# Two fp32r matmuls on the high and low parts of the sums of squares in place of one fp32 matmul

## The chip, the cores and the metric

The kernel runs on one core of a Trainium2 chip. The metric is the time of one execution on the device in microseconds (us); before the change three timed runs gave 1935.99, 1937.84 and 1938.87 us, median 1937.84. The engines are TensorE (PE, matmuls; its weight loads are listed as PEld), VectorE (DVE), ScalarE (ACT), GpSimd (POOL) and SyncE (SP), which issues most DMA transfers.

## The reference, cut to what matters

One decoder layer for 1024 prompt tokens and 64 sample tokens, width 1024: two SwiGLU feed-forward networks (FFN), and between them a mixer of windowed attention and a gated linear recurrence. Each of the three parts has a norm before it and a norm behind it, and all are root-mean-square norms:

```python
def rms_norm(x, g):
    xf = x.astype(jnp.float32)
    y = xf * lax.rsqrt(jnp.mean(xf * xf, axis=-1, keepdims=True) + EPS)
    return (y * g.astype(jnp.float32)).astype(x.dtype)

def run_layer(x, ...):
    x = x + 0.5 * rms_norm(swiglu(rms_norm(x, norm_ffn1_pre), ffn1_w_gu, ffn1_w_down), norm_ffn1_post)
    h = rms_norm(x, norm_mix_pre)
    ...
    x = x + rms_norm(mix, norm_mix_post)
    x = x + 0.5 * rms_norm(swiglu(rms_norm(x, norm_ffn2_pre), ffn2_w_gu, ffn2_w_down), norm_ffn2_post)
```

## The kernel before

The tokens are cut into three groups: group 0 has 320 (256 prompt tokens and the 64 samples), groups 1 and 2 have 384 each. Each large product is made of three matmuls (`mm3`, lines 260 to 262): a number is split into a high part of the type fp32r and the fp32r rest, and high times high, high times low and low times high are added up in a bank of PSUM. `split` (lines 238 to 241) makes the parts: a cast on ACT for the high one, a subtraction on DVE (or POOL) for the low one. Weights arrive in raw tiles over SP's queue and are split the same way.

Group 0 is kept feature-major for most of the program, with features on the partitions and tokens in the columns, and so are groups 1 and 2 before the first FFN. There a norm has to sum over partitions. `bcast_steps` (line 313) squares the eight blocks of 128 features on ACT and adds them up on DVE (on POOL for groups 1 and 2) in a tile `ss` of 128 rows; `mean_root` (line 290) multiplies `ss` by `omean`, a matrix that holds 1/1024 everywhere, which gives every partition the mean of all squares, and takes the root's inverse with a few steps on DVE and ACT (lines 297 to 305). The matmul by `omean` is an fp32 one (line 295). It stands at eight places: in the opening (`pre_first`, group 0), in the two norms of groups 1 and 2 before the first FFN (`pre_x`), behind and before the first FFN and the mixer (`post_t`, `pre_t`, group 0, four places) and at the end (`post_t`).

What sets the order: the norms' code runs as generators in named streams. `tick()` is called after each piece of a product and lets a stream go on to its next `yield`, so the number of `yield`s sets between which products a step of a norm stands; `need(name)` runs a stream to its end. The code written so is then put in order engine by engine by a scheduler that works with its own time simulation. In `pre_first` the order of the opening is written by hand: `order` and `after` chain the instructions of an engine. The small tiles (`ss`, `sq`, `rt`, `mt`, `mq`, and those of the gates, `sg` and `su`) share a ring of eight buffers with the tag "t2".

The opening makes six products of 320 columns with weights 0 to 5; their banks are read by `gated0` (lines 718 and 725) as soon as the root `rb` is there. Up to 138 us the gate and up products of group 0 follow, and beside them `factor` (lines 469 and 471) makes the operands of the two other groups for a multiplication of seven instead of eight products. The second matmul of the FFN for groups 1 and 2 starts about 570 us (weights `w`, activations `ar`), and beside it the stream `c0` runs `post_t` and `pre_t` for group 0, with residual sums on POOL (line 349).

Of the kernel before, what the change touches and what calls it, by code (L numbers as in the profile page):

```python
# [8 lines left out]
F32 = mybir.dt.float32  # L9
F32R = mybir.dt.float32r  # L10
# [4 lines left out]
ALU = mybir.AluOpType  # L15
# [3 lines left out]
P = 128  # L19
D = 1024  # L20
# [27 lines left out]
def tile_step(ctx: ExitStack, tc: tile.TileContext, A: dict, O: list):  # L48
    nc = tc.nc
    V, S, G, PE = nc.vector, nc.scalar, nc.gpsimd, nc.tensor  # L50

    cp = ctx.enter_context(tc.tile_pool(name="cp", bufs=1))
    pp = ctx.enter_context(tc.tile_pool(name="pp", bufs=1))
# [5 lines left out]
    def uid(s):  # L59
        cnt[0] += 1  # L60
        return f"{s}_{cnt[0]}"
# [4 lines left out]
    def axbank(s="ax"):  # L66
        return ps.tile([P, 512], F32, tag="ax", bufs=4, name=uid(s))
# [55 lines left out]
    ones = cp.tile([P, P], F32, name="ones")  # L123
    V.memset(ones, 1.0)
    junk = cp.tile([P, 512], BF16, name="junk")
    omean = cp.tile([P, P], F32, name="omean")
    V.memset(omean, 1.0 / D)
    S.activation(junk[:, :P], ones, AF.Silu)
    cols = cp.tile([P, NROWS], F32, name="cols")
    f1pre = cp.tile([P, KC], F32, name="f1pre")  # L130
# [106 lines left out]
    made = {}  # L237

    def split(hi, lo, src, lo_eng=None):
        made['S'] = S.copy(hi, src).ins  # L240
        (lo_eng or V).tensor_tensor(lo, src, hi.bitcast(F32), op=ALU.subtract)  # L241
# [16 lines left out]
    def mm3(out, a, b, first, last, resume=False):  # L258

        PE.matmul(out, a[0], b[0], start=first, stop=False, skip_group_check=resume)  # L260
        PE.matmul(out, a[0], b[1], start=False, stop=False, skip_group_check=resume)  # L261
        return PE.matmul(out, a[1], b[0], start=False, stop=last, skip_group_check=resume).ins  # L262
# [24 lines left out]
    def tmp2(name, shape=(P, 512)):  # L287
        return pp.tile(list(shape), F32, tag="t2", bufs=8, name=uid(name))

    def mean_root(ss, dst=None):  # L290
        w = ss.shape[-1]
        bank = axbank("rb")
        y = tmp2("rt")[:, :w]
        x = bank[:, :w]
        made = PE.matmul(x, omean, ss, start=True, stop=True)
        t = tmp2("mt")[:, :w]
        V.tensor_scalar(y.bitcast(I32), x.bitcast(I32), -0.5, float(MAGIC), op0=ALU.mult, op1=ALU.add)
        S.activation(t, y, AF.Square)
        V.tensor_tensor(t, x, t, op=ALU.mult)
        V.scalar_tensor_tensor(y, t, -3.0 * RS ** 2, y, op0=ALU.add, op1=ALU.mult)  # L300
        S.activation(t, y, AF.Square)
        V.tensor_tensor(t, x, t, op=ALU.mult)
        q = tmp2("mq")[:, :w]
        V.scalar_tensor_tensor(q, t, -40.0 / 3 * RS ** 6, t, op0=ALU.add, op1=ALU.mult)
        end = V.scalar_tensor_tensor(x if dst is None else dst, q, 80.0 * RS ** 12, y, op0=ALU.add, op1=ALU.mult)
        return made, x, end

    def sum_squares(E, ss, sq, d):
        if d == 1:
            return V.scalar_tensor_tensor(ss, ss, EPS * D / P, sq, op0=ALU.add, op1=ALU.add)  # L310
        return E.tensor_tensor(ss, ss, sq, op=ALU.add)

    def bcast_steps(part, w, out, add=None):

        ss = tmp2("ss")
        for d in range(KC):
            if d == 0:
                S.activation(ss[:, :w], part(d), AF.Square)
                continue
            sq = tmp2("sq")  # L320
            S.activation(sq[:, :w], part(d), AF.Square)
            sum_squares(G if add else V, ss[:, :w], sq[:, :w], d)
            if d % 3 == 0 or add:
                yield
        yield
        if add:
            yield
            yield
        rb = mean_root(ss[:, :w])[1]
        yield  # L330
        yield
        out.append(rb)
        yield
# [248 lines left out]
    def pre_first(x, gpre, h, raws, wts):  # L582
# [3 lines left out]
        w = WIDTH[0]  # L586
# [8 lines left out]
        def order(e, made):  # L595
            last[e] = made.ins
            return made

        def after(e):
            return tc.issue_after(last[e]) if e in last else nullcontext()  # L600
# [23 lines left out]
        def products(bank, n, ks):  # L624
            for k in ks:
                with after("PE"):
                    last["PE"] = mm3(bank[:, :w], (tiles[n][0][:, k, :], tiles[n][1][:, k, :]), hcol(h[0], k, w),
                                     k == 0, k == KC - 1)

        ss = tmp2("ss")[:, :w]  # L630

        def squares(ds):
            for d in ds:
                sq = tmp2("sq")[:, :w] if d else ss
                with after("S"):
                    order("S", S.activation(sq, x_part(d), AF.Square))
                if d:
                    with after("V"):
                        order("V", sum_squares(V, ss, sq, d))
# [18 lines left out]
        squares(range(2, 5))  # L658
        weight(4, 0, KC)
        squares(range(5, 8))  # L660
        products(banks[1][0], 2, range(KC))
        products(banks[1][1], 3, range(7))
        weight(5, 0, KC)
        rb = tmp2("rb")[:, :w]
        with after("PE"), after("V"), after("S"):
            made = mean_root(ss, rb)
        order("PE", made[0])
        order("V", made[2])
        products(banks[1][1], 3, range(7, KC))
# [1245 lines left out]
```

## Time and profile before

| | us |
|---|---|
| timed runs, median (lowest to highest) | 1937.84 (1935.99 to 1938.87) |
| profiled execution: span from first to last instruction | 1937.4 |
| PE busy | 1923.1 |
| PE's weight loads busy | 1806.1 |
| DVE busy | 1430.7 |
| ACT busy | 946.0 |
| POOL busy | 186.1 |

For the profiled execution the span is the only time that is recorded. The page cuts the span into 40 equal slices:

```profile
PE   9999999999999999999999999999999999999998
DVE  6896789877568666787678758756987887656666
ACT  5553444444455434545445545846544444445452
PEclk9999999999999999999999999999999999999999
```

Each digit is the busy share of a slice in tenths (9 is 90% or more); PEclk is the clock granted to TensorE, in tenths of its full speed. PE is busy from end to end at full clock. Matmuls are pipelined, and their recorded durations overlap: what one costs in a stream is read from the start of one to the start of the next.

### The profile page before, as it was taken

The numbers are of one execution on the slowest core, as the hardware profiler recorded it, in microseconds if no ns is written. First come the engines' busy times: TensorE is split into PE (matmuls) and PEld (weight loads), VectorE is DVE, ScalarE is ACT, GpSimd is POOL, SyncE is SP. The second block draws the span as 40 slices with busy tenths as digits, with TensorE's granted clock in tenths as the row PEclk, the third lists the DMA queues.
The fourth block names the chain that finished last, engine by engine and source line by source line (L and its number), as shares of the span: only waits on it lengthen the run. The fifth ranks groups of instructions, "written<-read, shape, count | busy, mean of one in ns | idle before, by whom it ended". The sixth has DMA issues, their size and how long they took to land.

```text
span 1937.4 us, 34843 instructions
## 1 busy us (share of the span) xinstructions
PE 1923.1 (99%) x13547; PEld 1806.1 (93%) x13547; DVE 1430.7 (74%) x2469; ACT 946.0 (49%) x1701; POOL 186.1 (10%) x227
## 2 busy tenths in 40 slices
PE   9999999999999999999999999999999999999998
PEld 9999999999998987788999888989999999999886
DVE  6896789877568666787678758756987887656666
ACT  5553444444455434545445545846544444445452
POOL 0300000000004022020221212000000000000102
PEclk9999999999999999999999999999999999999999
DMA  6643676555767556765334344546555555667974
GB/s 248 209 133 115 232 267 247 206 191 184 242 217 242 180 155 215 283 220 163 114 102 153 99 140 142 164 147 209 185 198 192 198 188 189 210 228 241 308 255 141
DMA packets 175750, 375.56 MB, mean 194 GB/s; under 512 B 16144, under 2 KB 67536, under 8 KB 175568
## 3 DMA queue, kind: packets, MB, share of 16 engines
q1 hardware_dynamic: 169680, 362.84, 56.0%
q10 hardware_dynamic: 5904, 10.49, 1.5%
q8 instruction: 106, 1.74, 0.4%
q14 instruction: 60, 0.49, 0.1%
HBM read 290.86 MB, written 83.39 MB: 193 GB/s over the span
## 4 chain that ended last, share of the span: by engine, by line
PE 88%; DMA 6%; DVE 3%; ACT 1%; issue 1%; POOL 1%; SPq 0%; ACTq 0%; DVEq 0%; POOLq 0%
PE mm L260 27%; PE mm L262 26%; PE mm L261 26%; DMA ar<-fa 1%; DMA xt<-in_x_rest_dram 1%; DMA ar<-act 1%; PE lv L1337 1%; PE sc L1237 1%; DMA raw<-in_ffn_w_gu_dram 1%; PE pv L1283 1%; DVE w L241 1%; PE pT L1269 1%; PE c L262 0%; PE c L260 0%; PE c L261 0%
## 5 line engine op out<-in xcount | busy, mean ns | idle before, releaser
L260 PE MATMUL mm<-h,wsph 128*128 128x320 f32 (+1 forms) x1344 | 427.2, 319 | 0.4 <-DVE big L814 0.4
L261 PE MATMUL mm<-h,wsph 128*128 128x320 f32 (+1 forms) x1344 | 425.5, 317 | 0.2 <-DVE h L241 0.2
L262 PE MATMUL mm<-h,wspl 128*128 128x320 f32 (+1 forms) x1344 | 422.6, 316 | 0.0
L241 DVE TENSOR_TENSOR wspl<-raw,wsph 128x1024 fp32r<-128x1024 f32 x208 | 260.8, 1255 | 125.2 <-ACT wsph L240 124.1
L240 ACT CAST wsph<-raw 128x1024 fp32r<-128x1024 f32 x208 | 217.8, 1049 | 254.0 <-PE mm L261 199.3
L260 PEld LDWEIGHTS mm<-h,wsph 128*128 128x128 f32 x1344 | 252.2, 188 | 4.2 <-issue 2.3
L261 PEld LDWEIGHTS mm<-h,wsph 128*128 128x128 f32 x1344 | 252.5, 188 | 3.9 <-issue 2.3
L262 PEld LDWEIGHTS mm<-h,wspl 128*128 128x128 f32 x1344 | 251.9, 188 | 3.4 <-issue 3.1
L240 ACT CAST w<-raw 128x512 fp32r<-128x512 f32 (+1 forms) x208 | 153.8, 745 | 199.9 <-PE mm L261 96.2
L261 PE MATMUL mm<-h,w 128*128 128x384 f32 (+1 forms) x736 | 245.6, 334 | 0.3 <-DVE h L622 0.3
L260 PE MATMUL mm<-h,w 128*128 128x384 f32 (+1 forms) x736 | 245.7, 334 | 0.2 <-ACT h L620 0.2
L262 PE MATMUL mm<-h,w 128*128 128x384 f32 (+1 forms) x736 | 239.6, 333 | 0.5 <-POOL w L613 0.4
L241 DVE TENSOR_TENSOR w<-raw,w 128x512 fp32r<-128x512 f32 (+1 forms) x208 | 178.3, 861 | 72.6 <-ACT w L240 71.7
L261 PE MATMUL mm<-w,h 128*128 128x512 f32 x462 | 180.5, 391 | 0.7 <-DVE w L241 0.7
L260 PE MATMUL mm<-w,h 128*128 128x512 f32 x462 | 180.8, 394 | 0.0
L262 PE MATMUL mm<-w,h 128*128 128x512 f32 x462 | 179.8, 391 | 0.0
L260 PE MATMUL mm<-big,w 128*128 128x384 f32 x528 | 176.7, 335 | 0.3 <-ACT big L806 0.2
L261 PE MATMUL mm<-big,w 128*128 128x384 f32 x528 | 176.5, 334 | 0.0
L262 PE MATMUL mm<-big,w 128*128 128x384 f32 x528 | 176.0, 334 | 0.0
L261 PEld LDWEIGHTS mm<-h,w 128*128 128x128 f32 x736 | 138.1, 188 | 1.1 <-DVE h L622 0.8
L260 PEld LDWEIGHTS mm<-h,w 128*128 128x128 f32 x736 | 138.1, 188 | 0.8 <-ACT h L620 0.5
L262 PEld LDWEIGHTS mm<-h,w 128*128 128x128 f32 x736 | 137.6, 188 | 1.0 <-POOL w L613 0.7
(367 smaller groups left out, 3353.8 us busy)
## 6 DMA issues: line engine op xcount, KB each, us to landing
raw<-in_ffn_w_gu_dram SPq DMA_DIRECT2D x162, 512.0 KB
raw<-in_ffn_w_down_dram SPq DMA_DIRECT2D x74, 512.0 KB
raw<-in_w_in_dram SPq DMA_DIRECT2D x54, 512.0 KB
ar<-fa SPq DMA_DIRECT2D x70, 384.0 KB
big<-in_ffn_w_down_dram SPq DMA_DIRECT2D x88, 256.0 KB
fb<-big SPq DMA_DIRECT2D x44, 512.0 KB
fa<-big SPq DMA_DIRECT2D x22, 768.0 KB
raw<-fb SPq DMA_DIRECT2D x30, 512.0 KB
```

Of the source, the lines that this page charges most:

```text
L240: made['S'] = S.copy(hi, src).ins
L241: (lo_eng or V).tensor_tensor(lo, src, hi.bitcast(F32), op=ALU.subtract)
L260: PE.matmul(out, a[0], b[0], start=first, stop=False, skip_group_check=resume)
L261: PE.matmul(out, a[0], b[1], start=False, stop=False, skip_group_check=resume)
L262: return PE.matmul(out, a[1], b[0], start=False, stop=last, skip_group_check=resume).ins
L1237: PE.matmul(banks[g][rows(hq), i, cs], zq[rows(g), 2 * pr + i, b * P + 64 * hq:b * P + 64 * hq + 64], kx[rows(g), k0 + cs.start:k0 + cs.st ...
L1269: PE.transpose(tb2[hq][:, g, i, slot], pt[g][rows(hq), c:c + P], ident[rows(hq), rows(hq)])
L1283: PE.matmul(ob[par][rows(g), :, hq], vn[rows(par), b + (blk + hq) // 2, rows(g)], pT[hq][rows(par), g, :, PLACE[hq][blk]], start=alone or ...
L1337: PE.matmul(b5[32 * i:32 * i + 32, b, a], K[:, a, cs], Q[:, a, cs], start=True, stop=True)
```

## The change

`omean` gets the type fp32r. The sums `ss` are split into two fp32r parts `ms`, a cast on ACT and a subtraction on DVE, and two matmuls by `omean` add both into the same bank. In `bcast_steps` the split stands one step behind the last square, and the matmuls two or three steps behind the split: each norm has one `yield` more before its matmul. In the opening the split is written behind the last square and ahead of the products with weights 2 and 3 in the code's order; on ACT and DVE it so comes ahead of the sixth weight tile (number 5).

```diff
-    omean = cp.tile([P, P], F32, name="omean")
-    V.memset(omean, 1.0 / D)
+    omean = cp.tile([P, P], F32R, name="omean")
+    V.memset(omean.bitcast(F32), 1.0 / D)
...
-    def mean_root(ss, dst=None):
-        w = ss.shape[-1]
+    def mean_parts(w):
+        return [pp.tile([P, 512], F32R, tag="t2", bufs=8, name=uid("ms"))[:, :w] for _ in range(2)]
+
+    def two_parts(ss):
+        parts = mean_parts(ss.shape[-1])
+        split(*parts, ss)
+        return parts
+
+    def mean_root(parts, dst=None):
+        w = parts[0].shape[-1]
         bank = axbank("rb")
         y = tmp2("rt")[:, :w]
         x = bank[:, :w]
-        made = PE.matmul(x, omean, ss, start=True, stop=True)
+        PE.matmul(x, omean, parts[0], start=True, stop=False)
+        made = PE.matmul(x, omean, parts[1], start=False, stop=True)
...
             if d % 3 == 0 or add:
                 yield
+        if add:
+            yield
+        parts = two_parts(ss[:, :w])
+        yield
         yield
         if add:
             yield
-            yield
-        rb = mean_root(ss[:, :w])[1]
+        rb = mean_root(parts)[1]
...
         squares(range(5, 8))
+        with after("S"):
+            order("S", S.copy(parts[0], ss))
+        with after("V"):
+            order("V", V.tensor_tensor(parts[1], ss, parts[0].bitcast(F32), op=ALU.subtract))
         products(banks[1][0], 2, range(KC))
         products(banks[1][1], 3, range(7))
         weight(5, 0, KC)
         rb = tmp2("rb")[:, :w]
         with after("PE"), after("V"), after("S"):
-            made = mean_root(ss, rb)
+            made = mean_root(parts, rb)
```

The scheduler then places instructions anew. PE keeps its other instructions, and their order up to small shifts of the attention's pieces among the products. Two places are shown, one row for an instruction (or several alike), in the order of the engine. The first is DVE in the opening, from the last three sums of squares (`ss`) on; `w_313` is the low part of the sixth weight tile, `rt` the first step of the root. Before:

```order
L311 TENSOR_TENSOR ss_146<-ss_146,sq_258 128x320
L311 TENSOR_TENSOR ss_146<-ss_146,sq_261 128x320
L311 TENSOR_TENSOR ss_146<-ss_146,sq_264 128x320
L613 TENSOR_TENSOR w_313<-big_109,w_312 128x1024
L145 TENSOR_SCALAR halfpost<-cols 128x8
L146 TENSOR_SCALAR halfpost<-cols 128x8
L150 TENSOR_SCALAR nsinkb<-nsinkb 128x8
L201 TENSOR_TENSOR lbe<-cols 128x4
L297 TENSOR_SCALAR rt_318<-rb_317 128x320
```

With the change (its lines are numbered anew: 320 is the old 311, 625 the old 613, 306 the old 297):

```order
L320 TENSOR_TENSOR ss_146<-ss_146,sq_260 128x320
L320 TENSOR_TENSOR ss_146<-ss_146,sq_263 128x320
L320 TENSOR_TENSOR ss_146<-ss_146,sq_266 128x320
L677 TENSOR_TENSOR ms_148<-ss_146,ms_147 128x320
L145 TENSOR_SCALAR halfpost<-cols 128x8
L146 TENSOR_SCALAR halfpost<-cols 128x8
L150 TENSOR_SCALAR nsinkb<-nsinkb 128x8
L201 TENSOR_TENSOR lbe<-cols 128x4
L202 TENSOR_TENSOR lbe<-cols,lbe 128x4
L203 TENSOR_TENSOR lbe<-cols,lbe 128x4
L625 TENSOR_TENSOR w_317<-big_109,w_316 128x1024
L306 TENSOR_SCALAR rt_322<-rb_321 128x320
```

The subtraction `ms` has come between the sums and the small constants, and the sixth weight tile's low part, which stood before those constants, now stands right ahead of the root's first step.

The second place is ACT about 580 to 592 us, where the second matmul of the first FFN runs: `w` are casts of its weights, `h` of its activations, `ss` and `sq` the squares of the norm `pre_t`, which wait for POOL's residual sums. Before:

```order
L240 CAST h_6177<-ar_6178 128x2x384
L240 CAST w_6034<-raw_6032 128x1024
L318 ACTIVATE ss_6021<-big_5069 128x320
L240 CAST h_6214<-ar_6215 128x384
L321 ACTIVATE sq_6023<-big_5069 128x320
L321 ACTIVATE sq_6026<-big_5069 128x320
L321 ACTIVATE sq_6029<-big_5069 128x320
L321 ACTIVATE sq_6055<-big_5070 128x320
L240 CAST w_6087<-raw_6085 128x1024
L240 CAST h_6243<-ar_6244 128x2x384
L321 ACTIVATE sq_6058<-big_5070 128x320
L1014 COPY big_5802<-mm_5803 128x512
```

With the change (327 and 330 are the old 318 and 321, 1031 the old 1014):

```order
L240 CAST w_6041<-raw_6039 128x1024
L310 ACTIVATE mt_5939<-rt_5936 128x320
L240 CAST h_6231<-ar_6232 128x384
L240 CAST w_6098<-raw_6096 128x1024
L240 CAST h_6268<-ar_6269 128x2x384
L1031 COPY big_5817<-mm_5818 128x512
L1031 COPY big_5817<-mm_5819 128x512
L240 CAST w_6141<-raw_6139 128x1024
L1031 COPY big_5817<-mm_5820 128x512
L240 CAST h_6297<-ar_6298 128x2x384
L327 ACTIVATE ss_6064<-big_5084 128x320
L330 ACTIVATE sq_6066<-big_5084 128x320
```

Before, five squares stood ahead of the cast of `w_6087`; now the cast that answers to it, `w_6098`, and the next one, `w_6141`, stand ahead of the first square.

## Rows read from the trace of the kernel before

**Rows 1.** The page's first lines: span, and busy time of each engine.
```profile
span 1937.4 us, 34843 instructions
...
PE 1923.1 (99%) x13547; PEld 1806.1 (93%) x13547; DVE 1430.7 (74%) x2469; ACT 946.0 (49%) x1701; POOL 186.1 (10%) x227
```

**Rows 2.** The page's chain of waits, by engine and by line.
```profile
PE 88%; DMA 6%; DVE 3%; ACT 1%; issue 1%; POOL 1%; SPq 0%; ACTq 0%; DVEq 0%; POOLq 0%
PE mm L260 27%; PE mm L262 26%; PE mm L261 26%; DMA ar<-fa 1%; DMA xt<-in_x_rest_dram 1%; DMA ar<-act 1%; PE lv L1337 1%; PE sc L1237 1%; DMA raw<-in_ffn_w_gu_dram 1%; PE pv L1283 1%; DVE w L241 1%; PE pT L1269 1%; PE c L262 0%; PE c L260 0
```

**Rows 3.** Who PE waited for: us in total, times, longest.
```profile
PE spT L1517 <- ACT t L1512: 1.3, 1, 1.3
...
PE mm L261 <- DVE w L241: 0.7, 1, 0.7
```

**Rows 4.** The group of the tile omean: minimum, median, maximum in ns.
```profile
L295 PE MATMUL rb<-ss,omean x16: 430/432/590, 22.0 to 1780.9; 128*128 128x320 f32 x12, 128*128 128x384 f32 x4
```

**Rows 5.** Timeline of PE at 94 us: start, duration, engine, line, operation.
```profile
94.17 0.31 PE L262 MATMUL mm<-h,wspl 128*128 128x320 f32 x1
...
95.11 0.31 PE L261 MATMUL mm<-h,wsph 128*128 128x320 f32 x1
95.26 0.31 PE L262 MATMUL mm<-h,wspl 128*128 128x320 f32 x1
```

**Rows 6.** Timeline of PE at 1009 us.
```profile
1009.16 0.34 PE L260 MATMUL mm<-h,wsph 128*128 128x384 f32 x1
...
1010.05 0.33 PE L262 MATMUL mm<-h,wspl 128*128 128x384 f32 x1
1010.22 0.34 PE L260 MATMUL mm<-h,wsph 128*128 128x384 f32 x1
```

**Rows 7.** Groups by line: a DVE subtraction's like, and ACT's cast.
```profile
L311 DVE TENSOR_TENSOR ss<-ss,sq x36: 480/492/1157, 16.4 to 1774.8; 128x320 f32<-128x320 f32 x36
...
L240 ACT CAST h<-ht x16: 438/459/461, 609.2 to 1085.3; 128x320 fp32r<-128x320 f32 x16
```

**Rows 8.** Timelines of POOL and PE: w_in's operand, last piece and first reader.
```profile
619.83 0.87 POOL L241 TENSOR_TENSOR h<-ht,h 128x320 fp32r<-128x320 f32 x1
...
634.94 0.30 PE L260 MATMUL mm<-h,wsph 128*128 128x320 f32 x1
```

**Rows 9.** Timelines of DVE and PE in the opening.
```profile
19.09 1.68 DVE L311 TENSOR_TENSOR ss<-ss,sq 128x320 f32<-128x320 f32 x3
...
22.73 0.49 DVE L297 TENSOR_SCALAR rt<-rb 128x320 int32<-128x320 int32 x1 [0.53 <-PE rb L295]
...
27.98 0.48 DVE L718 TENSOR_TENSOR sg<-mm,rb 128x320 f32<-128x320 f32 x1
...
30.00 0.31 PE L260 MATMUL mm<-h,wsph 128*128 128x320 f32 x1
```

**Rows 10.** Timeline of PE's weight loads at 56 us, with what was waited for.
```profile
56.61 0.30 PEld L295 LDWEIGHTS rb<-ss,omean 128*128 128x128 f32 x2 [0.31 <-POOL ss L311]
```

**Rows 11.** Timelines of ACT, DVE and PE around 592 us.
```profile
589.23 0.47 ACT L321 ACTIVATE sq<-big 128x320 f32<-128x320 f32 x1 [0.68 <-POOL big L349]
...
590.67 1.53 DVE L241 TENSOR_TENSOR w<-raw,w 128x1024 fp32r<-128x1024 f32 x1 [1.13 <-ACT w L240]
...
590.89 0.39 PE L262 MATMUL mm<-w,h 128*128 128x512 f32 x1
591.12 0.39 PE L260 MATMUL mm<-w,h 128*128 128x512 f32 x1
592.25 0.50 PE L261 MATMUL mm<-w,h 128*128 128x512 f32 x1 [0.74 <-DVE w L241]
```

**Rows 12.** Busy time in a stretch: us, then each engine (instructions), clock, DMA.
```profile
110.00:140.00 30.00, 30.00 (x204) 30.00 (x203) 30.00 (x35) 16.54 (x21) 0.00 (x0) 1.00 0.44 134
```

**Rows 13.** Timelines of DVE and PE: the first weight after the gate phase.
```profile
134.40 1.29 DVE L241 TENSOR_TENSOR w<-raw,w 128x512 fp32r<-128x512 f32 x2
...
137.79 0.34 PE L260 MATMUL mm<-h,w 128*128 128x384 f32 x1
```

More of the change, by code (lines that the diff above doesn't have):

```diff
@@ L630, in pre_first @@
         ss = tmp2("ss")[:, :w]
+        parts = mean_parts(w)
         def squares(ds):
```

## The prediction

> **What bounds the kernel now.** I read the page's top first. The span is 1937.4 us and TensorE (PE) is busy for 1923.1 us of it [rows 1]; the reader is to see that nothing but TensorE's own stream can be shortened much. The chain of waits then puts 88% of the span on PE, nearly all of it the three-matmul products on lines 260 to 262 [rows 2]. The list of waits of PE is short: its longest single item is 1.3 us, and one of 0.7 us stands near a place of this change [rows 3]. So a microsecond counts only if it is taken out of PE's stream, or if a late operand puts a hole into it.
>
> The changed operation is one matmul, line 295, at eight places; the group by tile shows 16 records, two per place, of 430 to 590 ns [rows 4]. Records overlap, so I price it from start to start in the timeline. At 94 us the three-term stream of 320 columns runs at 0.147 us a matmul (95.11 to 95.26). The matmul of line 260 stands between the one of line 262 at 94.17 and the one of line 261 at 95.11: 0.94 us for two steps of 0.147, so line 295, 384 columns wide here, took 0.94 - 0.29 = 0.65 us [rows 5]. At 1009 us the same reading of a 320-column one, between products of 384 columns at 0.172 us a step, is 1010.05 - 1009.16 - 2 x 0.172 = 0.545 us [rows 6]. The other five 320-column places (22, 573, 600, 1055 and 1780 us) read alike give 0.535 to 0.55 us; the second 384-column place (56 us) has a wait in it and is priced like that of 94 us.
>
> **The change, part by part.** *The matmuls.* Each place loses 0.545 us (six times) or 0.65 us (twice) and gains two fp32r matmuls. Their kind, 128x128 weights with 320 or 384 columns in fp32r, is that of the stream around them: 0.147 or 0.172 us each [rows 5, 6]. Saved: 6 x (0.545 - 0.294) + 2 x (0.65 - 0.344) = 1.51 + 0.61 = 2.12 us, all on the path. The bounds of this term: no saving at all if a pair cost what the one did, and 2.2 us with the largest readings of line 295 (0.55 and 0.65) and the smallest of a step (0.144 and 0.17).
>
> The row says that the fp32 matmul costs 0.545 us against 0.147 us, a factor of 3.7. The Trainium skill, "FP8 and Floating Point Precision", section TensorE Precision Notes, says that a true fp32 product is made in four passes through the array, and a reduced fp32 in one. Four full steps would be 0.588 and 0.688 us, and the term would be 2.45 us instead of 2.12; I keep the measured start-to-start.
>
> *The splits.* Eight casts on ScalarE (ACT), about 0.46 us each at 320 columns, and eight subtractions on VectorE (DVE), about 0.49 us each [rows 7]: 3.7 and 3.9 us on engines that are busy 49% and 74% of the span [rows 1]. They lengthen each norm's chain by some 1.1 us with two hand-offs, and the streams give each norm one more step before the matmul. What hides this is the distance from a norm to its reader. For the norm before w_in, the last low part leaves POOL about 620.7 and PE first reads this tile at 634.94 [rows 8], 14 us; the printed order puts the second norm's matmul 35 to 42 products later than before, which at 0.23 us a product of 512 columns [rows 11] is up to 9.7 us. It still fits, by some 4 us; what didn't fit would be PE's wait. The norm before the second FFN has more room still by the same reading. The last norm, at 1780 us, feeds only an output.
>
> *The opening.* This is the tightest place. The sum of squares is complete at 20.77 us [rows 9]; then cast (0.09 hand-off + 0.46), hand-off 0.09 and subtraction 0.49 end at 21.9. PE comes to the first new matmul at 21.99 and to the second at 22.13, so it shouldn't wait; that is 0.2 us of room. But ACT now casts the sums before the sixth weight tile, and DVE subtracts before that tile's low part, as the order shows. So this 1.04 us cast starts at 21.3, the 1.22 us subtraction at about 22.4, and the first step of the root (line 297, in order behind it on DVE) starts at 23.6 instead of 22.73: 0.85 us late. Everything behind on DVE moves as well, and the first reading of a product's bank (line 718) goes from 27.98 to 28.8, ending at 29.3. The product that takes this bank next starts at 30.00, after the change at 29.75. There is 0.45 us left, and I cost this at nothing; every microsecond more on DVE's queue would be 0.5 us or more of PE waiting.
>
> *A wait that goes.* At 56 us PE's weight load waited 0.31 us for the POOL sum [rows 10]. The order now puts the first part 18 products (2.6 us) later, the second 27 products. The wait goes: -0.31 us.
>
> *A wait that may go.* At 592 us PE stands 592.25 - 591.12 - 0.23 = 0.90 us for the low part of a weight tile [rows 11]. Its cast stood on ACT behind five squares of a norm, which waited for POOL's residual sums. In the new order two weight casts more stand ahead of those squares, but the residual's loads stand behind one more load of right-hand sides on SP. I count this as zero, with bounds of -0.9 and +0.9 us.
>
> *Everything else* (one constant tile's type, two more buffers of the "t2" ring, the attention pieces shifted by 2 to 18 products) keeps the number and order of PE's other instructions. Zero, and I allow 1 us either way, the size of the longest waits there [rows 3].
>
> Sum: 2.12 + 0.31 = 2.43 us. Against the profiled execution's span this is 1937.4 - 2.4 = 1935.0; no time around the span is given for it, and the three timed runs (1935.99 to 1938.87) enclose it, with a median 0.44 us above. Taken from the median: **1935.4 us**, 0.13% less.
>
> **Rivals.** *A larger gain.* The wait at 592 us goes too: 2.43 + 0.90 = 3.3 us, 1934.5. For it: the casts' new place in ACT's order; against: the later loads on SP, and that squares now stand ahead of a later cast.
>
> *No gain from the swap.* Two accumulating matmuls of another kind of number could cost what the two records of the fp32 one do (0.43 us each, overlapping). Then only the 0.31 us is left: 1937.5. For it: the fp32 matmul is two loads and two matmul records already [rows 4], so the count of records doesn't fall. Against: fp32r pairs run at 0.147 us everywhere else in the trace.
>
> *VectorE's backlog, the case of slower.* From 110 to 140 us DVE is busy for 30.00 of 30.00 us [rows 12]: it makes the FFN's operand sums and their low parts, behind the second prompt norm at 94 us. That norm's matmul moves 24 products (3.5 us) later; less what is saved until then, the root starts some 2.9 us later, and DVE has two subtractions of 384 columns more, at most 0.6 us each (0.49 by 384/320). The first weight of the next phase is split on DVE at 134.40 and ready about 135.0; PE wants it at 137.79 [rows 13], 2.8 us of room. If all 2.9 + 1.2 = 4.1 us arrived there and DVE's queue behind it had no room either, PE would stand for 4.1 us in all: 4.1 - 2.4 = 1.7 us slower, 1939.5. It decides from the point where DVE's pieces for the next phase come more than 2.8 us later than before. Against it: the new order moves the last operand's split and one eviction behind this weight, and takes one weight split and two gate products ahead of the root; by my count of the queue the weight is ready no later than before.
>
> **How the numbers follow.** The forecast (1935.4, give or take 1) has 0.52, the larger gain 0.24, no gain from the swap 0.12, the backlog 0.12. About 0.2%, 3.9 us, is what a measurement of this kernel can tell from no change. Faster by more than that is under 1934.0: two fifths of the larger gain and a sixth of the forecast, 0.19. Slower by more is over 1941.7, which takes the backlog and 2 us of small waits on top: 0.05. Within: 0.76. The range: 1932.6 (the larger gain, 1 us of small waits fewer, and the 1 us by which the three runs lie around their median) to 1939.9 (the backlog and half a microsecond of these).
>
> **What would show it.** Right: line 295's sixteen records of 0.43 us and more are replaced by sixteen of 0.31 to 0.34 us, and PE takes 0.25 to 0.31 us less per place from start to start; no wait of PE on the new tile "ms"; the wait on POOL at 56 us is gone; PE's busy time falls by about 2 us. Wrong: PE waiting for line 675 or 677 at 22 us or for a bank at 29.8 us; PE waiting for weights or operands between 137 and 150 us; a new hole between 575 and 620 us; or more than 0.4 us from start to start for a pair.

## The result, and the profile after

| | before | after |
|---|---|---|
| median of the timed runs, us | 1937.34 (1935.99 to 1939.32, 14 runs) | 1942.44 (1938.12 to 1945.74, 14 runs) |
| span of the profiled execution, us | 1937.4 | 1940.2 |

The ratio after to before is 1.0023, 95% interval 1.0016 to 1.0031: about 4.5 us slower by the ratio, 5.1 between the medians. The forecast was 1935.4, with 1939.9 as the upper end of the range. The sign was wrong. The changed kernel's runs also spread over 7.6 us, those of the kernel before over 3.3. Where a run has both, the time is 1.7 us more than the span (1941.87 and 1940.2 for the profiled execution of the changed kernel); by this the profiled execution of before took an estimated 1939.1 us, 1.8 above its median, and that of the changed kernel is 0.6 below its own. The two traces so show 2.8 us of the 5.1.

The place of the gain and of the loss can be read by following one instruction through both traces. The rows are the starts of the first matmul of a stretch, which does the same work in both kernels; what changes from row to row was won or lost between them, in one execution of each.

| first matmul of | before, us | after, us | difference |
|---|---|---|---|
| the gate stage's last operand sums | 130.46 | 129.58 | -0.88 |
| the last change of operands ahead of the down products | 516.07 | 513.87 | -2.20 |
| w_in for the samples [rows 8] | 634.94 | 631.45 | -3.49 |
| the down products after it | 684.54 | 685.99 | +1.45 |
| the down products after the second w_in | 1135.20 | 1138.65 | +3.45 |
| the last of the FFN's head | 1389.40 | 1392.38 | +2.98 |

So up to 631 us the changed kernel was 3.5 us ahead, more than I had forecast for the whole program. 4.9 us were then lost between 635 and 685 us, and another 2 us between 685 and 1135 us.

Not all of the 3.5 us is the change's. 1.3 us of it were won between 130 and 516 us, where no changed matmul stands: short waits of PE in the trace of before (0.17 us for line 806 at 305.69, 0.18 for line 241 at 486.62 and 0.44 for line 814 at 496.31, and a step 0.3 us too long at 291) are gone or shorter. The two profiles of e2 below, one kernel, have some of them in one and fewer in the other, so they come and go with the execution.

*What was won.* The page's top answers to [rows 1]; the span has grown by 2.8 us and PE is busy 1.5 us longer, where I had forecast about 2 us less.

```profile
span 1940.2 us, 34852 instructions
...
PE 1924.6 (99%) x13547; PEld 1809.1 (93%) x13547; DVE 1434.9 (74%) x2477; ACT 948.4 (49%) x1709; POOL 193.4 (10%) x227
```

PE's timeline at 22 us (320 columns) and at 97 us (384 columns, [rows 5]) shows the pairs: start, duration, engine, line, operation.

```profile
22.26 0.31 PE L303 MATMUL rb<-ms,omean 128*128 128x320 f32 x1
...
22.55 0.31 PE L260 MATMUL mm<-h,w 128*128 128x320 f32 x1
...
97.26 0.34 PE L303 MATMUL rb<-ms,omean 128*128 128x384 f32 x1
...
97.61 0.31 PE L260 MATMUL mm<-h,wsph 128*128 128x320 f32 x1
```

A pair takes 22.55 - 22.26 = 0.29 us and 97.61 - 97.26 = 0.35 us from start to start, as forecast. Before, one matmul took 0.545 and 0.65 us.

*The first loss.* Who PE waited for [rows 3] now begins with a wait that was not there:

```profile
PE mm L260 <- DVE big L1028: 3.2, 1, 3.2
```

Line 1028 (1011 before) is the eviction (the reading of a bank, which frees it) of the three banks of the down product with number 6 of seven: `V.tensor_tensor(y1[1][:, i], bank, y1[0][:, i], op=ALU.add)`. The product ring has four banks; w_in's first projection takes the fourth, its second needs the first of these three. PE's timeline there, and the granted clock by stretches (us, busy us, instructions, weight loads, VectorE, ACT, POOL, then the clock):

```profile
634.82 0.31 PE L262 MATMUL mm<-h,wspl 128*128 128x320 f32 x1
638.29 0.61 PE L260 MATMUL mm<-h,wsph 128*128 128x320 f32 x1 [3.16 <-DVE big L1028]
638.70 0.47 PE L261 MATMUL mm<-h,wsph 128*128 128x320 f32 x1
...
641.82 0.31 PE L261 MATMUL mm<-h,wsph 128*128 128x320 f32 x1
```

```profile
635.00:640.00 5.00, 1.84 (x7) 1.74 (x7) 3.53 (x6) 3.89 (x7) 0.00 (x0) 0.83 0.66 224
640.00:645.00 5.00, 5.00 (x30) 5.00 (x30) 5.00 (x7) 4.62 (x9) 1.22 (x1) 0.83 0.77 232
```

The step into 638.29 is 3.47 us instead of 0.147, 3.32 us lost. Behind it the matmuls start 0.266 us apart instead of 0.147: TensorE runs at the lower of its two levels (1.2 instead of 2.4 GHz; the mean of these two stretches is 0.83, and 1.00 in the one before and the one behind) until about 641.7. From 638.29 to 641.82 there are 13 steps; at 0.147 they would take 1.91 us and not 3.53, another 1.62 us. Together 4.9 us, the whole of the first loss.

*Why the eviction was late.* VectorE, ACT, POOL and SP of the changed kernel in the 35 us before, one fence each:

```profile
617.45 0.96 DVE L241 TENSOR_TENSOR h<-ar,h 128x768 fp32r<-128x768 f32 x1 [4.52 <-ACT h L240]
...
620.05 3.76 DVE L379 SCALAR_TENSOR_TENSOR ht<-big,cols,rb 128x320 f32<-128x320 f32 x8
...
629.96 1.62 DVE L241 TENSOR_TENSOR h<-ar,h 128x768 fp32r<-128x768 f32 x1
...
636.59 0.96 DVE L241 TENSOR_TENSOR h<-ar,h 128x768 fp32r<-128x768 f32 x1 [1.47 <-ACT h L240]
637.46 0.68 DVE L1028 TENSOR_TENSOR big<-mm,big 128x512 f32<-128x512 f32 x1
```

```profile
616.58 0.83 ACT L240 CAST h<-ar 128x768 fp32r<-128x768 f32 x1 [6.84 <-DMA ar<-fa]
617.32 0.47 ACT L310 ACTIVATE mt<-rt 128x320 f32<-128x320 f32 x1
...
635.72 0.83 ACT L240 CAST h<-ar 128x768 fp32r<-128x768 f32 x1 [2.32 <-DMA ar<-fa]
```

```profile
623.41 9.75 POOL L241 TENSOR_TENSOR h<-ht,h 128x320 fp32r<-128x320 f32 x7
```

```profile
607.22 1.72 SPq L1103 DMA_DIRECT2D aon<-in_attn_out_norm_dram  x1
609.00 0.43 SPq L1105 DMA_DIRECT2D bhi<-in_b_in_dram  x1
609.51 0.38 SPq L1015 DMA_DIRECT2D ar<-fa  x1
```

And of the kernel before, ACT and then VectorE:

```profile
604.43 0.47 ACT L301 ACTIVATE mt<-rt 128x320 f32<-128x320 f32 x1
```

```profile
608.58 3.75 DVE L367 SCALAR_TENSOR_TENSOR ht<-big,cols,rb 128x320 f32<-128x320 f32 x8
...
633.93 0.96 DVE L241 TENSOR_TENSOR h<-ar,h 128x768 fp32r<-128x768 f32 x1 [1.91 <-ACT h L240]
634.81 0.68 DVE L1011 TENSOR_TENSOR big<-mm,big 128x512 f32<-128x512 f32 x1
```

PE's timelines of the matmuls of this norm, before and then after, show how little of the delay is the place:

```profile
600.13 0.70 PE L295 MATMUL rb<-ss,omean 128*128 128x320 f32 x2
```

```profile
604.50 0.31 PE L303 MATMUL rb<-ms,omean 128*128 128x320 f32 x1
...
606.26 0.31 PE L304 MATMUL rb<-ms,omean 128*128 128x320 f32 x1
```

The reader is to see a chain. The norm's matmuls come 4.4 and 6.1 us later, but its second square (line 310; 301 before) is at 617.32 instead of 604.43, 12.9 us later: it now stands behind a cast of a right-hand side (`ar`) in ACT's order, whose load was issued behind two others and kept ACT standing for 6.84 us. That cast itself is 2.3 us later than before (616.58 against 614.26) and 0.5 to 2.3 later than in e1, e2 and e3 below, where the square stands ahead of it. The norm's eight results leave VectorE at 620 to 624 instead of 609 to 612 us, and their low parts keep POOL busy without a break from 623.4 to 633.2. In that time VectorE's subtraction of 768 columns takes 1.62 us instead of 0.96. VectorE gives the raw buffers back later, SP loads later, and the fifth right-hand side, behind which the eviction stands in both orders, is cast at 635.72 instead of 633.05. The eviction starts at 637.46 instead of 634.81, 2.65 us late, for a PE that is 3.49 us early. That each of these steps is needed is read from the order and the waits; the experiments test the place, the splitting and POOL.

*The second loss.* The attention's score matmuls (line 1254, 1237 before) come in groups of eight (16 records, two for each fp32 matmul) of 64x64 weights: four read the upper and four the lower half of the partitions. PE's timeline of the same group, before and then after; in the changed kernel products stand between the two halves:

```profile
1027.19 0.83 PE L1237 MATMUL sc<-kx,big 64*64 64x192 f32 x16
1027.95 0.44 PE L262 MATMUL mm<-h,wspl 128*128 128x384 f32 x1
```

```profile
1027.90 0.82 PE L1254 MATMUL sc<-kx,big 64*64 64x192 f32 x8
1028.66 0.44 PE L262 MATMUL mm<-h,wspl 128*128 128x384 f32 x1
...
1031.66 0.87 PE L1254 MATMUL sc<-kx,big 64*64 64x192 f32 x8
1032.46 0.49 PE L1471 MATMUL av<-big,big 128*128 128x128 f32 x2
```

Together the eight take 1027.95 - 1027.19 = 0.76 us. Apart, each half takes as long as both: 0.76 and 0.80. The trace of before has three such split groups (740, 968 and 1163 us), that of after has six (1028, 1076 and 1092 us besides). Adding up start to next start, the 128 score records of 192 columns from 786 to 1136 us take 7.07 us before and 9.45 after: +2.38. Two pairs in this stretch (1009 and 1055 us before) give back some 0.5, which leaves the 2 us of the table. PE's busy time for these matmuls alone, before and after, says the same:

```profile
680.00:1300.00 620.00, 15.63 (x256) 1.00 0.51 161
```

```profile
680.00:1300.00 620.00, 18.20 (x256) 1.00 0.49 160
```

### The profile page after: what moved, and what is told of

It reads as the page before. It is cut to its first block, busy times and chain, and to the rows that moved or that the text cites. A ratio compares the mean times of both kernels' runs of the same rounds, so it can differ in the third digit from the quotient of the medians.

```text
span 1940.2 us, 34852 instructions
## 1 busy us (share of the span) xinstructions
PE 1924.6 (99%) x13547; PEld 1809.1 (93%) x13547; DVE 1434.9 (74%) x2477; ACT 948.4 (49%) x1709; POOL 193.4 (10%) x227
## 4 chain that ended last, share of the span: by engine, by line
PE 92%; DMA 4%; DVE 2%; ACT 1%; issue 1%; SPq 0%; POOL 0%; ACTq 0%; DVEq 0%; POOLq 0%
PE mm L260 28%; PE mm L261 28%; PE mm L262 28%; DMA ar<-fa 2%; DMA xt<-in_x_rest_dram 1%; PE sc L1254 1%; DMA ar<-act 1%; PE lv L1354 1%; PE pv L1300 1%; PE pT L1286 1%; DVE h L241 1%; PE c L260 0%; PE c L262 0%; PE c L261 0%; DMA x1N<-big 0%
## 5 line engine op out<-in xcount | busy, mean ns | idle before, releaser
L240 ACT CAST wsph<-raw 128x1024 fp32r<-128x1024 f32 x208 | 217.5, 1048 | 242.2 <-PE mm L261 183.3
L240 ACT CAST w<-raw 128x512 fp32r<-128x512 f32 (+1 forms) x208 | 153.8, 745 | 190.4 <-PE mm L261 92.1
```

## The experiments

Each is compared with the kernel before on the same chip (median 1937.34 for the changed kernel, 1937.48 to 1937.76 for the others). Differences between two experiments are of medians.

| run | median, us | ratio to before, 95% | split groups | wait near 635 us in the profile |
|---|---|---|---|---|
| changed kernel | 1942.44 | 1.0016 to 1.0031 | 6 | 3.2 |
| e1 later place, no split sums | 1940.16 | 1.0004 to 1.0022 | 6 | none |
| e2 split sums, old place | 1935.36 | 0.9982 to 0.9999 | 3 | none |
| e3 c0's first pair of norms at the old place | 1938.40 | 0.9998 to 1.0016 | 6 | none |
| e4 score chain | 1941.06 | 1.0010 to 1.0032 | 7, one matmul apart | 2.4 |
| e5 second square on VectorE | 1939.42 | 1.0004 to 1.0022 | 6 | 1.9, at 644 us |
| e7 halves one behind the other | 1934.27 | 0.9975 to 0.9993 | 3 | none |
| e8 low parts on VectorE | 1939.03 | 0.9996 to 1.0015 | 6 | 2.0, at 643 us |
| e9 halves held together | 1934.86 | 0.9978 to 0.9995 | 0 | none |
| e10 e3 with halves held | 1936.25 | 0.9986 to 1.0004 | 1 | none |
| e11 before with halves held | 1937.56 | 0.9992 to 1.0010 | 0 | none |

**e1: the place alone.** The fp32 matmul of before, one step more:

```
+        if add:
+            yield
+        yield
         yield
         if add:
-            yield
             yield
         rb = mean_root(ss[:, :w])[1]
```

> The fp32 matmul and no splitting; only the extra step of the norms' streams before the matmul, so that the printed order of PE is that of the changed kernel (norm matmul 24 products later at 600 us, six split groups of score matmuls instead of three). Theory (the place of the norm and what it does to the order cost the time): PE stands about 3 us for a bank near 635 us with some us at the lower granted clock behind it, score groups of the attention at 1030, 1077 and 1093 us cost 0.8 us more each, and the time is that of the changed kernel plus the 2.1 us that the pairs save, 1942 to 1946. Rival (the casts and subtractions of the splitting load VectorE and make the hole): no hole at 635 us, 1937 to 1939.5.

1940.16 us, between the two expectations: under the theory's 1942 and over the rival's 1939.5. The score groups cost their 2.38 us (busy for 18.20 us, as in the changed kernel); there was no hole at 635 us, as the rival had it. ACT's timeline shows why: without cast and subtraction the norm is a little earlier, and both squares are ahead of the cast of `ar`.

```profile
607.43 0.47 ACT L301 ACTIVATE mt<-rt 128x320 f32<-128x320 f32 x1 [1.90 <-DVE rt L300]
...
614.37 0.83 ACT L240 CAST h<-ar 128x768 fp32r<-128x768 f32 x1 [2.92 <-DMA ar<-fa]
```

The theory that the place alone makes the hole is refuted. The rival is right on the hole and wrong on the time, since the place alone does split the score groups. With e2 below, the splitting without the later place, it follows that the hole takes both together.

**e2: the split sums, at the old place.**

```
         parts = two_parts(ss[:, :w])
         yield
-        yield
         if add:
             yield
         rb = mean_root(parts)[1]
```

> The two fp32r matmuls and the splitting, but with as many steps before the matmul as before, so that the norm's matmuls stand 576 products in, and three split score groups, as before. Theory: no hole at 635 us, no split groups more; what is left is the saving of the pairs: before minus 2.1 to 2.5 us, 1934 to 1936. Rival (the splitting's casts and subtractions make the hole): PE waits at 635 us again, 1940 or more.

1935.36 us, inside the expected interval: no hole, three split groups, 2.1 us under before. PE's longest wait is one of before [rows 3], 1.3 us, and a small one for the new cast has come (it is taken up below):

```profile
PE rb L303 <- ACT ms L240: 0.5, 1, 0.5
```

**A second profile of e2.** The kernel is that of e2, split opening included, whatever the label says.

> The kernel of the run with as many steps before the matmul as before, once more for a second profile of it: is its freedom from a hole at 635 us, and the 0.3 us that PE lost in the opening, there again? Theory: no wait over 1 us at 635 us, three split score groups, span 1933 to 1937. Rival (the hole comes and goes from run to run in this order too): a wait of 2 us or more for a bank.

Again no hole, span 1933.0 us, one time of 1934.71. PE here comes to w_in at 631.45 us, exactly as early as in the changed kernel, and finds its banks, since the eviction starts at 630.73 and not at 637.46. PE's lead alone makes no hole. VectorE's timeline, then PE's at the place of the hole:

```profile
630.73 0.68 DVE L1027 TENSOR_TENSOR big<-mm,big 128x512 f32<-128x512 f32 x1
```

```profile
634.97 0.31 PE L260 MATMUL mm<-h,wsph 128*128 128x320 f32 x1
```

The two profiles of one kernel are 3.5 us apart, so a single span can't settle a difference of that size.

**e3: one step fewer in the two norms before w_in alone**, the later norms as changed.

```
-        yield
+        if not soon:
+            yield
         if add:
...
-post_t(y, x0_all, halfpost[:, 0:8], x1T), pre_t(y, g, hmix))
+post_t(y, x0_all, halfpost[:, 0:8], x1T, True), pre_t(y, g, hmix, True))
```

> The changed kernel, but with one step fewer before the matmul in the first norm of the stream before w_in (3468 products in, as before); the second still comes through 3581 products in. The later norms and the six split score groups stay as in the changed kernel. Theory with two separate losses: the hole at 635 us and the clock behind it go (4.9 us), the three split groups stay (2.4 us): before minus 2.2 plus 2.4, 1936.5 to 1938.5. Rival 1 (one loss, all from the hole): 1934 to 1936. Rival 2 (the loss is from the norms at 1010 and 1055 us alone): 1940 to 1943 as changed.

The expectation speaks of the first of the two norms; the edit moves both, and in the trace the second norm's matmul too is back (598.30 us, against 599.65 in e2 and 604.50 in the changed kernel). 1938.40 us, inside the interval for two separate losses, at its upper end. The hole and the clock behind it are gone (PE busy 15.00 of 15.00 us from 630 to 645 us at 1.00), the six split groups are there. The three kernels in a row give the sizes: e2 - before = -2.1, e3 - e2 = +3.0 for the later norms and their split groups, changed - e3 = +4.0 for the place of the two norms before w_in.

**e4: the eight score matmuls held in their written order**, each behind the one before it, in the changed kernel.

```
+                behind = None
...
-                            PE.matmul(banks[g][rows(hq), i, cs],
...
+                            with tc.issue_after(behind) if behind else nullcontext():
+                                behind = PE.matmul(banks[g][rows(hq), i, cs],
...
```

> The changed kernel, with the eight matmuls of a score group held in their written order (banks alternating), so that none of the two halves runs alone. Theory: a group that is split costs 0.8 us for each half instead of 0.8 us for both; three more of these cost the changed kernel 2.4 us and the three that were there before some 2 us. With a first matmul still alone, 3 to 4 us come back and the hole at 635 us stays: 1938 to 1940. Rival (the two halves don't run beside each other, and the difference is records): no change, 1941 to 1943.

1941.06 us, at the lower end of the rival's interval, over the theory's 1940: only 1.4 us came back, which the two kernels' intervals don't tell from nothing. The score records tell more: their busy time falls by 1.34 us (18.20 to 16.86 between 680 and 1300 us), against the rival, but by less than the theory had it. The first matmul (two records) still goes alone, for 0.42 us, and the other seven take as long as eight:

```profile
1026.15 0.48 PE L1256 MATMUL sc<-kx,big 64*64 64x192 f32 x2
...
1030.24 0.87 PE L1256 MATMUL sc<-kx,big 64*64 64x192 f32 x14
```

Also, a seventh group is now split. The hole stayed, 2.4 us long in this profile. It is 0.8 us shorter because PE comes to w_in 0.91 us later (632.36 against 631.45); the eviction starts at the same time (637.56 against 637.46).

**e5: the norm's second square on VectorE** (`V.tensor_tensor(t, y, y, op=ALU.mult)`) in the norm before w_in of the changed kernel, which puts the eviction behind four right-hand sides.

> The changed kernel, but the second square of the norm before w_in runs on VectorE. The printed order then has the first two evictions of the sum banks (line 1028 of the changed kernel) behind four right-hand sides on VectorE, where the changed kernel and the one before have them behind five; the norm's results are about as late as in the changed kernel, and the six split score groups stay. Theory (PE stands near 635 us because the eviction waits behind the fifth right-hand side, whose load came late): the eviction of the first bank starts by about 634 to 635 us, PE waits under 1 us there and the clock stays: changed minus 4 to 5 us, 1937 to 1939. Rival (the late norm itself, whose low parts PE reads, makes the hole): PE waits 2 us or more, 1941 to 1944.

1939.42 us, 3 us better than the changed kernel, just over the interval. The wait for the bank is gone, but another stands in its place 9 us later, for an eviction (line 1138) further down VectorE's queue; PE also waits 1.2 us for the norm's cast (`PE rb L303 <- ACT ms L240`):

```profile
PE vT L1158 <- DVE t L1138: 1.9, 1, 1.9
```

So VectorE's queue is late as a whole (the first of the eight results is at 621.43 us); which instruction PE meets first is a matter of its order.

**e8: the low parts on VectorE instead of POOL**, changed kernel.

```
-            split(hi, lo, t[:, :w], G)
+            split(hi, lo, t[:, :w], V if h is hmix else G)
```

> The changed kernel, with the eight low parts of the norm before w_in made on VectorE instead of POOL. Theory (VectorE's subtractions took 1.6 to 1.9 us instead of 0.95 to 1.2 between 623 and 633 us because POOL worked beside it): they take 0.95 to 1.25 us again, which pays for the eight of 0.5 us; with four right-hand sides ahead of the first eviction the hole at 635 us shrinks under 1.5 us, 1937 to 1940. Rival (VectorE was slow there for lack of data, or its eight more subtractions delay the eviction as much): the subtractions keep 1.4 us or more, or PE waits 2 us or more, 1941 or more.

1939.03 us. With POOL idle VectorE's subtractions are back at 0.95 us (768 columns) and 1.22 us (1024, at 629.91):

```profile
625.63 0.95 DVE L241 TENSOR_TENSOR h<-ar,h 128x768 fp32r<-128x768 f32 x1
```

The eviction (633.92) is in time, and as in e5 PE waits 2.0 us for the later one. It also stands behind four right-hand sides here and not five, as the expectation says, so POOL's part in the delay can't be told from that of the order. Theory and rival each got a part: VectorE's subtractions were slow beside POOL, and VectorE's backlog doesn't go away by taking POOL's work over.

**e7: the halves always one behind the other**, on e2: the loop over the two halves (`g`) is put outside, and the eight are chained.

> The kernel with as many steps before the matmul as before, with the four score matmuls of one 64-row half always written and issued ahead of the four of the other half, in all groups. Theory (two halves of the array work side by side only where their matmuls alternate): the groups that alternated, sixteen of 64x192 or 64x128, go from 0.81 to some 1.6 us each, the three split ones stay: plus 12 us, 1946 to 1949. Rival (the split groups cost more for another reason, such as the bank that they wait for): no more than 2 us slower, under 1938.

1934.27 us, and the theory is refuted: written and issued apart, but with nothing between them, the eight take what they took in alternation (1009.57 - 1008.75 = 0.82).

```profile
1008.75 0.89 PE L1255 MATMUL sc<-kx,big 64*64 64x192 f32 x16
1009.57 0.44 PE L260 MATMUL mm<-h,wsph 128*128 128x384 f32 x1
```

So alternation isn't needed for the halves to run beside each other; in all the split groups matmuls of all 128 rows stand between. The rival, no more than 2 us slower, held. That it is 1.1 us faster than e2 is not explained; the two intervals overlap.

**e9, e10, e11: halves held together by a small matmul.** A one-column matmul takes the first bank ahead of the eight, so that they can all start when the second is free:

```
+                if pr:
+                    behind = PE.matmul(banks[0][rows(0), 0, cs.start:cs.start + 1], ..., start=True, stop=True).ins
...
+                        for g in ((1, 0) if pr else (0, 1)):
+                            with tc.issue_after(behind) if pr else nullcontext():
...
```

e9 is e2 with it:

> The kernel with as many steps before the matmul as before, and in the second score group of each block a one-column matmul into the first bank ahead of the eight score matmuls, which are then held in alternating order and start with the second bank: no product can come between the two halves. In the printed order no group is split (three were). Theory (four score matmuls with a product behind them take 0.75 to 0.80 us, and eight together 0.81): the three groups give back 0.53 to 0.79 us each, 2.0 us, less eleven one-column matmuls of an estimated 0.05 to 0.1 us: 1 to 1.5 us under the kernel without it, 1933.5 to 1934.5. Rival (the wait for the second bank comes back as a wait of PE): 1935 to 1937.

e10 is e3 with it:

> The changed kernel with one step fewer before the matmul in the two norms of the stream before w_in (run e3), and with the halves of the score groups held together as in the run before this one: one of the six split groups is left. Theory (what this kernel had over the one with all norms early, 3.0 us, is the three more split groups): five groups give back some 3.5 us less 0.5 to 1 us for the one-column matmuls: 1935.4 to 1936.2. Rival (the later norms at 1010 and 1060 us cost by themselves): 1937 or more, with a wait of PE or longer products there.

e11 is the kernel before with it:

> The kernel before, fp32 matmul and all, with the halves of the score groups held together: no group is split (three were). Theory: the same 1 to 1.5 us as from the kernel with the split sums, 1936.0 to 1936.6, and the two savings add up. Rival (the gain hangs on the order that the split sums made): 1937 or more.

PE's busy time for score matmuls in e9, e10 and e11, over the same stretch as above:

```profile
680.00:1300.00 620.00, 14.58 (x272) 1.00 0.51 161
```

```profile
680.00:1300.00 620.00, 15.78 (x272) 1.00 0.51 161
```

```profile
680.00:1300.00 620.00, 14.57 (x272) 1.00 0.50 161
```

e10 speaks for the split groups: 2.4 us of score time less than e3 (18.20 to 15.78), and 1938.40 - 1936.25 = 2.15 us of the whole, though the two intervals overlap a little. What e3 had over e2 is therefore, as far as medians tell, for the most part the split groups. Its 1936.25 is just above the expected interval. e9 and e11 save 1.05 us of score time against e2 and before (15.63 to 14.58 and 14.57); in the whole 0.5 and 0.2 us are seen, not to be told from nothing. e9's 1934.86 is just above the theory's interval, e11's 1937.56 inside the rival's: that the saving adds up without the split sums isn't shown. In their profiles PE waits 1.4 us (e9) and 0.5 us (e11) near 773 us for an eviction (line 1027 in e9, 1011 in e11), a wait that e2 and before don't have, so part of the saving came back much as e9's rival had it; this was not followed further. A one-column matmul, estimated at 0.05 to 0.1 us in the expectation of e9, took 0.10 us with the eight behind it (the group at 804 us, 0.86 us against 0.76 in e2) and 0.15 where a product stands behind it (737.42). e2, e7 and e9 beat the kernel before and the changed one, and can't be told from each other.

## Why the prediction was wrong

*The matmuls: right.* 0.29 and 0.35 us a pair against forecasts of 0.294 and 0.344. That e2 as a whole is 1937.49 - 1935.36 = 2.1 us under before is no second proof of the term of 2.12: the interval allows 0.2 to 3.5 us, and in e2 the wait at 592 us is gone as well and one of 0.5 us at 60 us has come. The factor of 3.7 between an fp32 matmul and a step of the stream is measured. Of the passes that I quoted from the Trainium skill, "FP8 and Floating Point Precision", TensorE Precision Notes, the page states the four of a true fp32 product; that a reduced one takes one pass was my reading of it, and no run here counts passes.

*The opening: right.* The cast, the subtraction and the first step of the root came where forecast (line 306 at 23.68 us, forecast 23.6; line 735 at 28.91, forecast 28.8), and PE doesn't wait at 30 us (the product that takes the bank starts at 30.03).

*The wait that goes, at 56 us: half right.* POOL's sum isn't waited for any more, and this trace of the changed kernel has no wait there. But the new cast can take its place: e2 waits 0.5 us for it (`PE rb L303 <- ACT ms L240`, above), e5 1.2 us. Counted over runs, the 0.31 us is not safe.

*The wait that may go, at 592 us:* it is gone (PE busy 59.99 of 60 us from 570 to 630 us), the rival "a larger gain", which I gave 0.24. At w_in's start the changed kernel was 3.49 us ahead. That this is near the rival's 3.3 is luck: 3.3 is for all eight places, and with the five that lie ahead of w_in the rival makes 2.6 there; 1.3 us came from the short waits between 130 and 516 us.

*The step that failed first:* "For the norm before w_in ... It still fits, by some 4 us; what didn't fit would be PE's wait." I measured the way from the norm's last low part to its reader: 620.7 to 634.94 us, with 9.7 us to add. The norm did come 13 us later and POOL ended at 633.2, 1.7 us behind PE's first w_in matmul (631.45), so by that measure it did not fit. PE never waited for that tile even so, because the eighth low part is read last, by the matmul at 634.67: the measure was wrong too. PE waited for a bank. I had counted what reads the norm's result and not what is queued behind its steps: eight scalings and a root on VectorE, whose order next holds the evictions, and eight low parts on POOL that slow VectorE down. The margin that mattered was the eviction's: before, it started at 634.81 and PE needed the bank at 634.94 + 3.5 = 638.4, some 3 us after its end. The delay of 2.65 us and PE's own lead of 3.49 us took it away. Where the norm isn't late, the eviction moves along with the lead (630.73 in the second profile of e2) and the lead does no harm; behind the late norm it stayed, and the lead, which was nowhere in my sum, came on top. And I had let the delay be proportional, 0.23 us a product, where an in-order queue made it jump: the matmuls came 4.4 and 6.1 us later, the square 12.9, because it fell behind a cast that waited 6.84 us for a load.

*The step that failed second:* "Everything else (... the attention pieces shifted by 2 to 18 products) keeps the number and order of PE's other instructions. Zero, and I allow 1 us either way". The number, yes; the order, no. Three groups of score matmuls came apart, 0.8 us each, 2.4 us where I had allowed 1. The order of PE's instructions shows this without any time in it: sixteen score records in a row before, eight and eight with products between them after (1027.19 and 1027.90 above). I had looked at how far pieces moved, not at whether they stayed whole.

*The rivals:* the one that ended slower had the right kind, a backlog on VectorE that PE meets, at the wrong place (110 to 140 us, where PE lost nothing) and with nothing of the score groups; its 1939.5 is still 2.9 us under the measured median.

*The sum:* losses of 4.9 and 2.4 us against gains of 2.1 (the pairs), 0.3 and 0.9 us (the waits at 56 and 592 us) make 4.0 us slower; 4.5 to 5.1 were measured.

The Trainium skill bears on both failures. The matmuls of 64x64 weights overlap in two halves, 0.76 to 0.82 us for eight as for four; "TensorEngine Tiling (Array Packing)", Tiling Modes, says that different tiles can run their matmuls in parallel and that a change of the tiling mode drains TensorE. The traces of after and of e7 agree with the first; the drain by itself no run here shows. VectorE's two-operand subtraction goes from 0.95 to 1.62 us beside POOL's; "SBUF — State Buffer", Who interferes with whom, says that a VectorE instruction with two inputs in SBUF and a GpSimd instruction that reads it contend for one port. e8, where POOL is idle and the same subtraction takes 0.95, agrees.

*What stays open.* Why the changed kernel's runs spread over 7.6 us was not tried; the hole's length goes with PE's lead (3.2 us at a lead of 3.49, 2.4 at one of 2.58 in e4), and the granted clock behind it fell in one profile and not in the other, which would fit. That the cast of `ar` ahead of the second square is what makes the norm jump is read from the order and the traces (the square stands behind that cast in the changed kernel, e4 and e8, ahead of it in before, e1, e2 and e3), not from a kernel in which that cast alone was moved.

## What to carry to other kernels

When a step moves in a list-scheduled kernel, don't ask only when its reader comes; ask what stands behind it on each in-order engine, and which of that frees a bank or a buffer that PE wants. Add the lead that the change gives PE to the demand side of every margin whose supply doesn't move along with PE. And compare the two orders of PE's instructions for groups that came apart: small matmuls that share the array lost their overlap here where a full-size one came between.

## What the runs showed of the hardware that was not expected

- Four matmuls of 64x64 weights and 192 columns in fp32, alone on one half of the rows, take 0.75 to 0.80 us; eight on both halves 0.76 to 0.82; one alone 0.42; seven 0.80.
- VectorE's subtraction of 768 columns takes 0.95 us alone and 1.62 us while POOL subtracts 320 columns at a time without a break; POOL's takes 0.87 us alone [rows 8] and 9.75 / 7 = 1.39 us then. Both engines lose.
- TensorE's granted clock fell behind one wait and not behind another of like length: 0.83 over the ten us behind a wait of 3.2 us in the changed kernel, 0.72 over six us behind 1.9 us in e5, and 1.00 behind 2.4 us in e4 and 2.0 us in e8.
